# Five unused strips of SBUF that move where the tiles of a hybrid decoder layer begin

## The chip, the cores and the metric

The kernel runs on one core of a Trainium2 chip. The metric is the device time of one execution in microseconds (us): lower is better. The kernel before was timed in three runs, median 1544.72 us, from 1542.8 to 1545.76. Everything else that is told of time here was read from one profiled execution of it.

Words used below: TensorE (PE, "the array") multiplies a *stationary* block of up to 128 x 128, which is loaded into it first (a weight load, PEld), with a *moving* block that streams through it; the sum lands in PSUM. VectorE is DVE, ScalarE ACT, GpSimd POOL; SyncE (SP) issues DMAs. All operands of the array lie in SBUF, where each of 128 partitions has its own bytes; "a tile begins at byte b" means byte b of every partition.

## What is computed

One decoder layer on 512 tokens of width 1024, in float32. After a norm, one projection feeds a short gated convolution and a gated linear recurrence (4 heads, chunks of 32 tokens); their outputs go through an output projection and a residual. Then a feed-forward part picks, for each token, 16 of 16384 experts for each of 8 heads, by product keys:

```
h = rmsnorm(x, norm_mix);  proj = h @ w_in
x = x + concat(conv(...), hgrn2(...)) @ w_out
h2 = rmsnorm(x, norm_ffn)
scores = (h2 @ wq) . keys          # 8 heads x 2 halves x 128 keys
expert, gate = 16 best pairs of the two halves, softmax
y = sum over the 128 experts of a token: gate * gelu(h2 . u[expert]) * v[expert]
out = rmsnorm(x + y, norm_f)
```

## The kernel before

The 512 tokens are 4 blocks of 128. Block 0 takes the experts as written: GpSimd gathers the rows of `u` and `v` (`rows`, L671), VectorE multiplies and adds (L677, L685). Blocks 1 to 3 (384 tokens) are computed densely: all 16384 experts in 128 chunks of 128, with a gate that is zero for experts not picked.

The stages, in the order in which the array meets them:

- **Projections** (`proj`, `proj_mm`): 28 units of weights and 4 of `w_v`. Then the recurrence, in small matmuls, and the **output projection** (`out_mm`).
- **Queries and scores** (`query`, `scores`): 16 units, each followed by small float32 matmuls of `q` with `keys`.
- **First half of the dense experts** (`uchunk`): gelu(h2 U^T) for one chunk, 24 matmuls with 384 moving columns into `pa`. Between them stands the **gate stage** (`gate_m`, L652 and L653): 768 matmuls of 128 columns in float16, which make the matrix of gates from one-hot tiles `A`, `B1` and `B2`, and write it to DRAM (`Gd`).
- **Main loop** (`vchunk`, `vmm`): second half, 18 matmuls with 512 moving columns a chunk into six PSUM banks `y`. For its first 41 turns a `uchunk` stands in each turn too; after those it is `vmm` alone.
- At the end the residual and the last norm (`finish`).

Each large float32 product is made of three matmuls on a rounded part (`hi`, type float32r) and a rest (`lo`), by the helper `mm3` (L113 to L115):

```
PE.matmul(out, l[0], r[0], start=first, stop=False)
PE.matmul(out, l[0], r[1], start=False, stop=False)
PE.matmul(out, l[1], r[0], start=False, stop=last)
```

The second argument is the stationary block, the third the moving one. A row of a trace names them the other way round: `y<-whi,wh` has `whi` moving and `wh` stationary. Which tile plays which part differs from stage to stage, and the prediction turns on it:

| stage | matmuls | moving | stationary |
|---|---|---|---|
| projections, queries | 576 + 384 | `hThi/lo`, `h2Thi/lo`, 512 columns | `whi/lo` |
| the projection of v | 96 | `whi/lo`, 512 | `hThi/lo` |
| output projection | 192 | `whi/lo`, 512 | `mhi/lo` |
| first half (`pa`) | 3072 | `h2Thi/lo`, 384 | `whi/lo` |
| gate stage | 768 | `B1`, `B2`, 128, a step of 4 elements | `A`, the same step |
| second half (`y`) | 2304 | `whi/lo`, 512 | `wh`, `wl` |

`whi/lo` are made from a loaded unit `wraw` by `split`: ACT rounds (L97), DVE subtracts (L99). They have four buffers each; `wraw` is a ring of 4, 8, then 12 buffers, which the gathered rows share. In the main loop DVE multiplies a chunk's activations with its gates (L740), and ACT and DVE split the product into `wh` and `wl` (L743, L745).

The tiles lie in pools, one behind the other in the order in which `body` opens them: constants `cst`, `hp` (hT, h2T), `ws` (whi, wlo), `sm` (small vectors), `mp` (gl), and then pools that follow each other in the same place: those of the front part, those of the selection (`kp`, `rs`, `sp`, `s2`), and those of the main loop (`rm`, `vp`). Each tile is padded to a multiple of 32 bytes. So a few short tiles early on shift all that lie behind them. A scheduler sets the order of the instructions; it does so from their dependencies and estimated lengths.

Of the kernel before, what the change touches and what calls it, by code (L numbers as in the profile page):

```python
# [10 lines left out]
F32 = mybir.dt.float32  # L11
F32R = mybir.dt.float32r
F16 = mybir.dt.float16
# [8 lines left out]
P = 128  # L22
T = 512
# [3 lines left out]
H = 8  # L27
NHP = 2 * H
K = 16
# [24 lines left out]
def body(ctx, tc, a):  # L54
    nc = tc.nc
    V, S, G, PE = nc.vector, nc.scalar, nc.gpsimd, nc.tensor

    def sb(name, bufs=1, **kw):
        return ctx.enter_context(tc.tile_pool(name=name, bufs=bufs, **kw))
# [4 lines left out]
    sm = sb("sm", 2)  # L64
# [3 lines left out]
    def const(name, shape, dt=F32):  # L68
        return cst.tile(shape, dt, name=name)
# [4 lines left out]
    gmask = const("gmask", [P, P])  # L74
    scanm = const("scanm", [P, T])
    ones = const("ones", [P, 2])

    def gain(nm, j):
        return prm[:, PRM[nm] + j:PRM[nm] + j + 1]
# [22 lines left out]
    def wunit(src):  # L102
        raw = ring[0]()
        nc.sync.dma_start(out=raw, in_=src)
        return split(raw)
# [6 lines left out]
    def mm3(out, l, r, first, last):  # L112
        PE.matmul(out, l[0], r[0], start=first, stop=False)  # L113
        PE.matmul(out, l[0], r[1], start=False, stop=False)  # L114
        PE.matmul(out, l[1], r[0], start=False, stop=last)  # L115

    hT = (hp.tile([P, ND, T], F32R, tag="hi", name="hThi"), hp.tile([P, ND, T], F32R, tag="lo", name="hTlo"))
    x1d = dr.tile([NB, P, D], F32, name="x1d")
    h2d = dr.tile([P, D], F32, name="h2d")
# [16 lines left out]
    def big(tag, shape, dt=F32):  # L136
        return fp.tile(shape, dt, tag=tag, name=tag)

    # ---- (x * gain)^T; 1 / rms of a token multiplies what the projections give
    xT = [big(t, [P, 2, T]) for t in ("F", "K", "G", "E1")]  # L140
    for t, nm in ((prm, "prm"), (ident, "ident")):
        S.dma_start(out=t, in_=a[nm])
# [10 lines left out]
        V.scalar_tensor_tensor(hT[1][:, dc, :], t, gain("norm_mix", dc), hT[0][:, dc, :].bitcast(F32), op0=OP.mult,  # L153
                               op1=OP.subtract)

    # ---- projections
    def proj_mm(o, w, dc):
        sl = slice(dc * P, (dc + 1) * P)
        mm3(o, (w[0][:, sl], w[1][:, sl]), (hT[0][:, dc, :], hT[1][:, dc, :]), dc == 0, dc == ND - 1)
# [239 lines left out]
            c = conv_c(tb + 1)  # L399
            hgrn_mix(tb, os_)  # L400

    # ---- output projection, residual, ffn norm
    nfb = fp.tile([P, D], F32, tag="v", name="nfb")
    nc.sync.dma_start(out=nfb, in_=a["norm_ffn"].to_broadcast([P, D]))
    x1 = [big(t, [P, 2, D]) for t in ("F", "K")]
# [27 lines left out]
        S.activation(tmp(), res(tb, 0), AF.Square, accum_out=ms[:, 0, tb:tb + 1])  # L433
    po = [ps() for _ in range(NB)]
    wo = {i: wunit(a["w_out"][1, i]) for i in OORD}
    # ---- dense experts, first half: gelu(h2 @ U^T) of one chunk of 128 experts
    def uchunk(c):
        w = wunit(a["u_l"][c])
        o = psA.tile([P, T], F32, tag="a", name="pa")[:, :TD]
        for dc in range(ND):  # L440
            sl = slice(dc * P, (dc + 1) * P)
            mm3(o, (w[0][:, sl], w[1][:, sl]), (h2T[0][:, dc, P:], h2T[1][:, dc, P:]), dc == 0, dc == ND - 1)
        gl = mp.tile([P, TD], F32, tag="gl", name="gl", bufs=LAG + 1)
        S.activation(gl, o, AF.Gelu)  # L444
        if c < SPILL:
            S.dma_start(out=Ad[c], in_=gl)
        return gl
# [35 lines left out]
    wq0 = [wunit(a["wq"][i]) for i in range(2)]  # L483
    front.close()

    # ---- product keys
    kp = sb("kp")
    e_i32 = kp.tile([P, H * K], I32, name="e_i32")
    gate0 = kp.tile([P, H * K], F32, name="gate0")
# [9 lines left out]
    sp = sel.enter_context(tc.tile_pool(name="sp", bufs=1))  # L499
# [5 lines left out]
    keys = sp.tile([P, NHP, NK], F32, name="keys")  # L505
    S.dma_start(out=keys, in_=a["keys"])
    iota4 = sp.tile([P, NK, 4], F16, name="iota4")
    S.dma_start(out=iota4, in_=a["iota4"])
    iota16 = sp.tile([P, K], F16, name="iota16")
    S.dma_start(out=iota16, in_=a["iota16"])  # L510
    topv = [sp.tile([P, H, 2, K], F32, name="tv%d" % tb) for tb in range(NB)]
    topi = [sp.tile([P, H, 2, K], U32, name="ti%d" % tb) for tb in range(NB)]
# [1 line left out]
    def top16(src, n, vout, iout):  # L514
        V.max(vout[:, 0:8], src)
        V.max_index(iout[:, 0:8], vout[:, 0:8], src)
        r = s2.tile([P, n], F32, tag="mr%d" % n, name="mr")
        V.match_replace(r, vout[:, 0:8], src, LOWEST)
        V.max(vout[:, 8:16], r)
        V.max_index(iout[:, 8:16], vout[:, 8:16], r)  # L520
# [18 lines left out]
            top16(s[:, tb, :], NK, topv[tb][:, i // 2, i % 2, :], topi[tb][:, i // 2, i % 2, :])  # L539

    def pick(tbs):
        """the 16 best pairs of keys of each head: gates and places of both keys.
        A pair (a, b) of the sorted keys has (a + 1) * (b + 1) - 1 others before it, so 50 pairs are all there are."""
        n = len(tbs) * H
        cf = sp.tile([P, len(tbs), H, K], F16, tag="cf", name="cf")
        gs = []
        for j, tb in enumerate(tbs):
            v1, v2 = topv[tb][:, :, 0, :], topv[tb][:, :, 1, :]
            cand = s2.tile([P, H, NCAND], F32, tag="B2", name="cand")
            for a0, st, m in ((0, 0, 16), (1, 16, 8), (2, 24, 5), (3, 29, 4), (4, 33, 3)):  # L550
                V.tensor_add(cand[:, :, st:st + m], v2[:, :, 0:m], v1[:, :, a0:a0 + 1].to_broadcast([P, H, m]))
            V.tensor_add(cand[:, :, 36:42].rearrange("p h (x y) -> p h x y", y=2),
                         v1[:, :, 5:8].unsqueeze(3).to_broadcast([P, H, 3, 2]),
                         v2[:, :, 0:2].unsqueeze(2).to_broadcast([P, H, 3, 2]))
            V.tensor_add(cand[:, :, 42:50], v1[:, :, 8:16], v2[:, :, 0:1].to_broadcast([P, H, 8]))
            cv = s2.tile([P, H, K], F32, tag="cv", name="cv")
            ci = s2.tile([P, H, K], U32, tag="ci", name="ci")
            for h in range(H):
                top16(cand[:, h, :], NCAND, cv[:, h, :], ci[:, h, :])
            g = sp.tile([P, H, K], F32, tag="g%d" % j, name="g")  # L560
            V.tensor_sub(g, cv, cv[:, :, 0:1].to_broadcast([P, H, K]))
            S.activation(g, g, AF.Exp)
            gsum = sp.tile([P, H], F32, tag="gsum", name="gsum")
            V.tensor_reduce(gsum, g, axis=AX.X, op=OP.add)
            V.reciprocal(gsum, gsum)
            V.tensor_mul(g, g, gsum.unsqueeze(2).to_broadcast([P, H, K]))
            gs.append(g.rearrange("p h k -> p (h k)"))
            V.tensor_copy(cf[:, j, :, :], ci)
        cf = cf.rearrange("p j h k -> p (j h k)")
        pa = sp.tile([P, n * K], F16, tag="pa", name="pa")  # L570
        pb = sp.tile([P, n * K], F16, tag="pb", name="pb")
        for j, (st, stp) in enumerate(zip(STARTS, STEPS)):
            m2 = s2.tile([P, n * K], F16, tag="B1", name="m2")
            if j:
                m = s2.tile([P, n * K], F16, tag="A", name="m")
                V.tensor_scalar(m, cf, float(st), None, op0=OP.is_ge)
                V.tensor_add(pa, pa, m)
            else:
                V.tensor_scalar(pa, cf, float(st), None, op0=OP.is_ge)
            V.tensor_scalar(m2, cf, float(st), float(stp), op0=OP.is_ge, op1=OP.mult)  # L580
            V.tensor_sub(pb, pb if j else cf, m2)
        V.scalar_tensor_tensor(pa, cf, -34.0, pa, op0=OP.add, op1=OP.max)
        V.scalar_tensor_tensor(pb, cf, 42.0, pb, op0=OP.is_lt, op1=OP.mult)
        return pa, pb, gs
# [43 lines left out]
    stg = {}  # L628

    def gate_m(tb, b):  # L630
        """gate matrix of 16 tokens: G[i1, i2] per token"""
        r = gt[tb]

        def view(j):
            return r[:, j, b * 16:(b + 1) * 16].rearrange("p (q t) -> p q t", t=4).unsqueeze(2).to_broadcast(
                [P, 4, NK, 4])
        io = iota4[:, None, :, :].to_broadcast([P, 4, NK, 4])
        A = s2.tile([P, 4, NK, 4], F16, tag="A", name="A")
        B1 = s2.tile([P, 4, NK, 4], F16, tag="B1", name="B1")
        B2 = s2.tile([P, 4, NK, 4], F16, tag="B2", name="B2")  # L640
        V.tensor_tensor(A, io, view(0), OP.is_equal)
        V.tensor_tensor(B1, io, view(1), OP.is_equal)
        V.tensor_mul(B2, B1, view(3))
        V.tensor_mul(B1, B1, view(2))
        if b % 2 == 0:
            stg[0] = s2.tile([P, NK // 4, 4, CH], F32, tag="stg", name="stg")
        st = stg[0].rearrange("p g c t -> p t (g c)")
        for q in range(4):
            o = ps()
            o3 = o.rearrange("p (t i) -> p t i", t=4)  # L650
            for t in range(4):
                PE.matmul(o3[:, t, :], A[:, q, :, t], B2[:, q, :, t], start=True, stop=False)  # L652
                PE.matmul(o3[:, t, :], A[:, q, :, t], B1[:, q, :, t], start=False, stop=True)  # L653
            t0 = (b % 2) * 16 + q * 4
            S.activation(st[:, t0:t0 + 4, :], o3, AF.Copy, scale=1.0 / GSC)  # L655
        if b % 2 == 1:
            blk = (tb - 1) * 4 + b // 2
            S.dma_start(out=Gd[:, :, blk].rearrange("g p c t -> p g (c t)"),
                        in_=stg[0].rearrange("p g c t -> p g (c t)"))
# [5 lines left out]
            scores(i - 1, prev)  # L665
        prev = q
    scores(NHP - 1, prev)
    # ---- block 0: rows of its experts gathered
    def rows(tab, j):
        t = ring[0]()  # L670
        G.indirect_dma_start(out=t, out_offset=None, in_=a[tab],  # L671
# [48 lines left out]
        gls[SPILL + k] = uchunk(SPILL + k)  # L720
    sel.close()

    # ---- main loop
    psY = sb("psY", 1, space=PSUM)
    raw_ring(sb("rm", 1), MRING)
    vp = sb("vp", 2)
# [49 lines left out]
        take(k)  # L776
    take(len(slots))

    # ---- residual and last norm
    nfb = vp.tile([P, D], F32, name="nfb", bufs=1)  # L780
    S.dma_start(out=nfb, in_=a["norm_f"].to_broadcast([P, D]))

# [76 lines left out]
```

## Time and profile before

| | us |
|---|---|
| median of three runs | 1544.72 |
| span of the profiled execution, first to last instruction | 1540.5 |
| TensorE busy in it | 1517.9 (99%) |
| VectorE busy | 1212.7 (79%) |
| ScalarE busy | 638.6 (41%) |
| GpSimd busy | 368.8 (24%) |

How to read it: the profile gives, for each instruction, its start and its end. A matmul's end is modelled and lies well behind the start of the next one, since matmuls follow each other in the array before the one ahead has left it. So "busy 99%" only says that the array was never left without work for long. How fast it works is read from starts: the distance from one matmul's start to the next one's is called its *pace* below.

### The profile page before, as it was taken

The page shows a single profiled execution, that of the slowest core. Times are in us where ns is not written, and L with a number is a line of the kernel's source. Part 1 is how long each engine was busy: PE and PEld are TensorE (multiplying, and loading weights), DVE is VectorE, ACT ScalarE, POOL GpSimd, SP SyncE. Part 2 cuts the span into 40 slices and gives each one's busy share as a digit, 9 for nine tenths or more (in the row PEclk, how much of TensorE's full clock was granted, in tenths as well). Part 3 has the DMA queues.
Part 4 walks back from the last instruction along what each step waited for, and adds up shares of the span by engine and source line. Part 5 has one row for each costly group of instructions (what it writes and reads, how often), then busy time and mean ns, then how long its engine had stood idle before and what let it go on. Part 6 is the DMA issues. An engine that isn't in the chain of part 4 may idle for free.

```text
span 1540.5 us, 21785 instructions
## 1 busy us (share of the span) xinstructions
PE 1517.9 (99%) x7929; PEld 1337.1 (87%) x7929; DVE 1212.7 (79%) x2312; ACT 638.6 (41%) x900; POOL 368.8 (24%) x300
## 2 busy tenths in 40 slices
PE   7999999999999999999999999999999999999997
PEld 6887777889999999999999998989898888888886
DVE  5846875899999987876738787777888788878787
ACT  5833334333443456466643333333333333333333
POOL 0000000000053231322014444444343233333340
PEclk9999999999999999999999999999999999999999
DMA  6221234523479787788679998999999999999983
GB/s 231 86 92 56 82 112 162 187 83 117 163 251 373 264 251 252 242 271 269 209 236 412 354 333 303 330 336 326 329 326 364 340 342 353 340 347 346 327 313 138
DMA packets 164653, 394.75 MB, mean 256 GB/s; under 512 B 13249, under 2 KB 84417, under 8 KB 164417
## 3 DMA queue, kind: packets, MB, share of 16 engines
q1 hardware_dynamic: 47520, 170.94, 30.7%
q0 software_dynamic: 41472, 159.40, 28.7%
q10 hardware_dynamic: 75552, 63.01, 12.8%
q8 instruction: 62, 1.02, 0.3%
q14 instruction: 47, 0.38, 0.1%
HBM read 346.90 MB, written 46.40 MB: 255 GB/s over the span
## 4 chain that ended last, share of the span: by engine, by line
PE 93%; DMA 2%; DVE 2%; ACT 1%; issue 1%; POOL 0%; ACTq 0%; DVEq 0%; SPq 0%; POOLq 0%
PE y L113 12%; PE y L114 12%; PE y L115 12%; PE pa L115 10%; PE pa L113 10%; PE pa L114 10%; PE pm L113 6%; PE pm L115 6%; PE pm L114 6%; PE pm L652 3%; PE pm L653 3%; PE pm L535 1%; PE pm L299 1%; DMA wraw<-in_u_dram,e_i 1%; DVE wlo L99 1%; DMA wraw<-in_v_l_dram 1%
## 5 line engine op out<-in xcount | busy, mean ns | idle before, releaser
L97 ACT ACTIVATE whi<-wraw 128x1024 fp32r<-128x1024 f32 x308 | 325.8, 1058 | 514.2 <-PE pa L114 197.9
L99 DVE TENSOR_TENSOR wlo<-wraw,whi 128x1024 fp32r<-128x1024 f32 x308 | 377.1, 1224 | 160.7 <-ACT whi L97 158.5
L113 PE MATMUL pa<-h2Thi,whi 128*128 128x384 f32 x1024 | 345.3, 337 | 2.5 <-ACT gl L444 2.5
L115 PE MATMUL pa<-h2Thi,wlo 128*128 128x384 f32 x1024 | 344.9, 337 | 0.3 <-DVE wlo L99 0.3
L114 PE MATMUL pa<-h2Tlo,whi 128*128 128x384 f32 x1024 | 344.5, 336 | 0.0
L114 PE MATMUL y<-wlo,wh 128*128 128x512 f32 x768 | 304.3, 396 | 0.0
L115 PE MATMUL y<-whi,wl 128*128 128x512 f32 x768 | 304.0, 396 | 0.0
L113 PE MATMUL y<-whi,wh 128*128 128x512 f32 x768 | 303.7, 397 | 0.0
L671 POOL DMA_INDIRECT wraw<-in_u_dram,e_i x128 | 174.9, 1366 | 492.5 <-DMA Ad<-gl 178.5
L671 POOL DMA_INDIRECT wraw<-in_v_dram,e_i x128 | 171.8, 1342 | 301.1 <-DVE wlo L99 136.9
L113 PEld LDWEIGHTS pa<-h2Thi,whi 128*128 128x128 f32 x1024 | 192.8, 188 | 6.0 <-ACT gl L444 3.7
L114 PEld LDWEIGHTS pa<-h2Tlo,whi 128*128 128x128 f32 x1024 | 192.8, 188 | 1.8
L115 PEld LDWEIGHTS pa<-h2Thi,wlo 128*128 128x128 f32 x1024 | 192.7, 188 | 0.9 <-DVE wlo L99 0.6
L115 PEld LDWEIGHTS y<-whi,wl 128*128 128x128 f32 x768 | 144.7, 188 | 35.4
L685 DVE SCALAR_TENSOR_TENSOR y<-wraw,w,y 128x1024 f32<-128x1024 f32 x128 | 163.8, 1280 | 13.8 <-DMA wraw<-in_v_dram,e_i 13.7
L743 ACT ACTIVATE wh<-w 128x384 fp32r<-128x384 f32 x128 | 67.1, 524 | 258.6 <-PE y L114 199.0
L113 PEld LDWEIGHTS y<-whi,wh 128*128 128x128 f32 x768 | 144.6, 188 | 33.2
L114 PEld LDWEIGHTS y<-wlo,wh 128*128 128x128 f32 x768 | 144.5, 188 | 33.2
L677 DVE SCALAR_TENSOR_TENSOR wraw<-wraw,h2n 128x1024 f32<-128x1024 f32 x128 | 155.9, 1219 | 18.7 <-DMA wraw<-in_u_dram,e_i 18.7
L745 DVE TENSOR_TENSOR wl<-w,wh 128x384 fp32r<-128x384 f32 x128 | 71.1, 556 | 53.0 <-ACT wh L743 52.6
L655 ACT ACTIVATE stg<-pm 128x512 f32<-128x512 f32 x96 | 94.3, 1161 | 19.5 <-PE pm L653 19.1
L652 PE MATMUL pm<-B,A 128*128 128x128 f16 x384 | 91.1, 296 | 0.2 <-ACT stg L655 0.2
(242 smaller groups left out, 1817.7 us busy)
## 6 DMA issues: line engine op xcount, KB each, us to landing
wraw<-in_u_l_dram SPq DMA_DIRECT2D x128, 512.0 KB, 5.3
wraw<-in_v_l_dram SPq DMA_DIRECT2D x128, 512.0 KB, 6.5
Gd<-stg ACTq DMA_DIRECT2D x12, 2048.0 KB, 9.9
Gt<-Gd POOLq DMA_DIRECT2D x32, 768.0 KB, 8.2
Ad<-gl ACTq DMA_DIRECT2D x84, 192.0 KB, 4.5
glr<-Ad ACTq DMA_DIRECT2D x84, 192.0 KB, 5.9
wraw<-in_w_in_dram SPq DMA_DIRECT2D x24, 512.0 KB, 3.7
wraw<-in_wq_dram SPq DMA_DIRECT2D x16, 512.0 KB, 8.3
```

What stands on the lines that cost most here:

```text
L97: S.activation(hi, src, AF.Copy)
L99: V.tensor_sub(lo, src, hi.bitcast(F32))
L113: PE.matmul(out, l[0], r[0], start=first, stop=False)
L114: PE.matmul(out, l[0], r[1], start=False, stop=False)
L115: PE.matmul(out, l[1], r[0], start=False, stop=last)
L652: PE.matmul(o3[:, t, :], A[:, q, :, t], B2[:, q, :, t], start=True, stop=False)
L655: S.activation(st[:, t0:t0 + 4, :], o3, AF.Copy, scale=1.0 / GSC)
L671: G.indirect_dma_start(out=t, out_offset=None, in_=a[tab], in_offset=bass.IndirectOffsetOnAxis(ap=e_i32[:, j:j + 1], axis=0))
L677: V.scalar_tensor_tensor(r, r, 1.0, h2n, op0=OP.mult, op1=OP.mult, accum_out=act0[:, j:j + 1])
L685: V.scalar_tensor_tensor(y0, r, w0[:, j:j + 1], y0, op0=OP.mult, op1=OP.add)
L743: S.activation(wh, w, AF.Copy)
L745: V.tensor_sub(wl, w, wh.bitcast(F32))
```

## The change

Five edits, none of which adds or removes an instruction, a wait or a transfer: two tiles that nothing reads or writes, and two tiles that are made wider than what is used of them. (Comments go as well; they move the line numbers by up to 2.)

```diff
     ones = const("ones", [P, 2])
+    const("pad", [P, 48])
...
+    sm.tile([P, 104], F32, name="pad", bufs=1)
     hT = (hp.tile([P, ND, T], F32R, tag="hi", name="hThi"), ...
...
-    iota16 = sp.tile([P, K], F16, name="iota16")
+    iota16 = sp.tile([P, K + 240], F16, name="iota16")[:, 0:K]
...
-            gsum = sp.tile([P, H], F32, tag="gsum", name="gsum")
+            gsum = sp.tile([P, P], F32, tag="gsum", name="gsum")[:, 0:H]
```

The built programs of both kernels have the same 13955 instructions in the same order on every engine, with the same semaphores and the same values waited for. What differs is where tiles begin. As a remainder after division by 512 bytes:

| tiles | before | after |
|---|---|---|
| `hThi/lo`, `h2Thi/lo`, `whi/lo` | 320 | 0 |
| `mhi/lo`, and all other tiles of the front part but `tmp` | 416 | 0 |
| `wraw`, `gl`, `h2n`, `y0`, `keys`, `glr`, `Gt`, `w` | 416 | 0 |
| `wh`, `wl` | 416 | 0 |
| `A`, `B1`, `B2`, `q`, `oh` | 224 | 256 |
| `stg`, `gt` | 160 | 192 |

The slices that a matmul reads begin at multiples of 512 bytes within their tile, so these remainders are those of the operands; only in the gate stage the four slices of a tile begin 0, 2, 4 and 6 bytes further on.

## Rows read from the trace of the kernel before

**Rows 1.** The page: span, busy us of each engine (share) and instructions, the chain by engine.
```profile
span 1540.5 us, 21785 instructions
...
PE 1517.9 (99%) x7929; PEld 1337.1 (87%) x7929; DVE 1212.7 (79%) x2312; ACT 638.6 (41%) x900; POOL 368.8 (24%) x300
...
PE 93%; DMA 2%; DVE 2%; ACT 1%; issue 1%; POOL 0%; ACTq 0%; DVEq 0%; SPq 0%; POOLq 0%
```

**Rows 2.** The waits of TensorE: waiter, releaser: total us, times, longest us.
```profile
PE pm L113 <- ACT whi L97: 8.3, 1, 8.3
PE pm L466 <- DVE h2s L459: 3.2, 2, 3.0
PE pa L113 <- ACT gl L444: 2.5, 2, 1.5
```

**Rows 3.** Windows, TensorE alone: stretch, length, busy (matmuls), granted clock, DMA share, GB/s.
```profile
60.00:78.00 18.00, 18.00 (x81) 1.00 0.34 115
216.00:236.00 20.00, 20.00 (x87) 1.00 0.16 54
410.00:426.00 16.00, 16.00 (x95) 1.00 0.55 172
1300.00:1320.00 20.00, 20.00 (x87) 1.00 0.92 333
820.00:840.00 20.00, 20.00 (x105) 1.00 1.03 408
```

**Rows 4.** Timeline of 60 to 78, projection of v: start, length (us), instruction.
```profile
59.70 0.39 PE L115 MATMUL pm<-whi,hTlo 128*128 128x512 f32 x1
...
77.83 0.39 PE L114 MATMUL pm<-wlo,hThi 128*128 128x512 f32 x1
```

**Rows 5.** Timeline of 216 to 236, output projection.
```profile
215.68 0.39 PE L113 MATMUL pm<-whi,mhi 128*128 128x512 f32 x1
...
235.83 0.40 PE L115 MATMUL pm<-whi,mlo 128*128 128x512 f32 x1
```

**Rows 6.** Timeline of 410 to 426, first half of the experts.
```profile
409.67 0.33 PE L113 MATMUL pa<-h2Thi,whi 128*128 128x384 f32 x1
...
425.96 0.33 PE L114 MATMUL pa<-h2Tlo,whi 128*128 128x384 f32 x1
```

**Rows 7.** Timeline of 1300 to 1320, second half of the experts.
```profile
1299.69 0.40 PE L113 MATMUL y<-whi,wh 128*128 128x512 f32 x1
...
1319.84 0.40 PE L115 MATMUL y<-whi,wl 128*128 128x512 f32 x1
```

**Rows 8.** Groups of TensorE by form: instruction, shapes, count | busy us, mean ns | idle.
```profile
L114 PE MATMUL y<-wlo,wh 128*128 128x512 f32 x768 | 304.3, 396 | 0.0
...
L114 PE MATMUL pm<-wlo,mhi 128*128 128x512 f32 x64 | 25.2, 396 | 0.0
...
L114 PE MATMUL pm<-wlo,hThi 128*128 128x512 f32 x32 | 12.4, 389 | 0.0
```

**Rows 9.** Timeline of the gate stage around 704.
```profile
704.02 0.29 PE L652 MATMUL pm<-B,A 128*128 128x128 f16 x1
704.14 0.41 PE L653 MATMUL pm<-B,A 128*128 128x128 f16 x2
...
704.96 0.30 PE L653 MATMUL pm<-B,A 128*128 128x128 f16 x1
```

**Rows 10.** Scores: the timeline around 325 (eight merged), and their group by form.
```profile
325.27 1.05 PE L535 MATMUL pm<-keys,q 128*128 128x128 f32 x8
...
L535 PE MATMUL pm<-keys,q 128*128 128x128 f32 x128 | 16.9, 275 | 0.0
```

**Rows 11.** Windows, all engines: PE, PEld, DVE, ACT, POOL busy (count), clock, DMA share, GB/s.
```profile
1200.00:1500.00 300.00, 300.00 (x1282) 241.17 (x1281) 243.11 (x321) 105.87 (x146) 102.73 (x93) 1.00 0.94 340
```

**Rows 12.** Groups of VectorE by form.
```profile
L99 DVE TENSOR_TENSOR wlo<-wraw,whi 128x1024 fp32r<-128x1024 f32 x308 | 377.1, 1224 | 160.7 <-ACT whi L97 158.5 <-PE pm L535 1.5
...
L677 DVE SCALAR_TENSOR_TENSOR wraw<-wraw,h2n 128x1024 f32<-128x1024 f32 x128 | 155.9, 1219 | 18.7 <-DMA wraw<-in_u_dram,e_i 18.7
```

## The prediction

> **What bounds the kernel now.** First the page: the array is busy for 1517.9 of 1540.5 us, and 93% of the chain that ended last is its own work [rows 1]. Next the waits, to see whether it is really work: the array waited 8.3 us at the start for the first weights, and then 3.2 and 2.5 us in two more places; these are its three longest sums [rows 2]. So no queue, transfer or other engine sets the time, and a change that moves no instruction can only act through the pace of the matmuls themselves.
>
> So the pace is read next, from starts, in four stretches that hold one kind of matmul each; the counts are those of the windows, and all four ran at a granted clock of 1.00, the level of 2.4 GHz [rows 3].
> - Projection of v: 81 matmuls of 512 columns, first start 59.70, last 77.83: 18.13 / 80 = 226.6 ns [rows 3, 4].
> - Output projection: 87 of 512 columns: (235.83 - 215.68) / 86 = 234.3 ns [rows 3, 5].
> - First half of the experts: 95 of 384 columns: (425.96 - 409.67) / 94 = 173.3 ns [rows 3, 6].
> - Second half: 87 of 512 columns: (1319.84 - 1299.69) / 86 = 234.3 ns [rows 3, 7].
>
> Two things come out. The difference of 226.6 and 173.3 for 128 columns is 0.416 ns a column, one cycle of 2.4 GHz. So a matmul of either width costs its columns and a constant: 226.6 - 213.3 = 13.3 ns, and 173.3 - 160.0 = 13.3 ns. And the output projection and the second half pay 21.0 ns, 7.7 ns more, though their shape and type are those of the projection of v. The mean lengths say the same: 396 ns for `y` and for the output projection, 389 for the projection of v [rows 8].
>
> What sets the two kinds apart? The moving operand is `whi/lo` in all three of the 512-column stretches, at 320 past a multiple of 512. The stationary one begins at 320 for the projection of v (`hThi/lo`), at 416 for the other two (`mhi/lo`, `wh`, `wl`). 320 is a multiple of 64, 416 is 32 past one. Other load is not the cause: the output projection is slow at a DMA share of 0.16, the projection of v fast at 0.34, and the second half slow, to the same tenth of a nanosecond, at 0.92 [rows 3].
>
> **The change, part by part.** The two strips take every fp32r operand to 0 past 512; then stationary and moving begin alike, as they do now in the projection of v. No instruction, wait or transfer is added or moved, so all else costs nothing of itself.
>
> *Second half of the experts.* 2304 matmuls, of which 768 are in the group shown (three such groups [rows 8]). From 234.3 to 226.6: 2304 x 7.7 = 17.7 us. All of it lies on the path: the array does not wait there [rows 2].
>
> *Output projection.* 192 matmuls, 192 x 7.7 = 1.5 us.
>
> *Projections, queries, first half.* 576 + 384 + 96 + 3072 = 4128 matmuls whose operands begin at a multiple of 64 already. That 0 past 512 is better still, no row shows; I take nothing. Bounds: at best all of the 13.3 ns, 54.9 us. At worst they lose what the 32 bytes cost elsewhere, 7.7 ns, 31.8 us; I see no ground for that, since both operands keep their distance to each other.
>
> *Gate stage.* 768 matmuls of 128 columns, nine starts from 704.02 to 704.96: 0.94 / 8 = 118 ns [rows 9]. 128 columns take 53 ns, so it is the load of the next stationary block that sets this pace. Both operands go from 224 (32 past a multiple of 64) to 256. The trace has no gate matmul at another place. The nearest row of 128 x 128 that is held up by as many columns is that of the scores: eight merged in 1.05 us, one is 0.275, so (1.05 - 0.275) / 7 = 111 ns [rows 10]. I take 118 - 111 = 7 ns, also close to the 7.7 above: 768 x 7 = 5.4 us. Bounds: 0, if the step of four elements is what costs, and 118 - 107 = 11 ns, 8.4 us, if the load comes down to 128 columns at half the array's rate (128 / 1.2 GHz).
>
> *The small float32 matmuls* of recurrence and scores stand at 111 ns, 107 of which are columns by the same sum: under 4 ns times some 400, at most 1.6 us, taken as 0.
>
> *Who is late next?* In the second half a chunk is 18 matmuls, 4.22 us now, 4.08 after. VectorE is busy 243.11 of 300 us there [rows 11], 0.81 x 4.22 = 3.42 us a chunk: 84% after, it still fits. The transfers run at 340 GB/s [rows 11], which becomes 340 x 4.22 / 4.08 = 352; they reach 408 at 820 to 840, where the DMA share stands at 1.03, full [rows 3]. So they fit as well; only in some 40 us after 800 could the array be held up, which might cost 1 to 2 us.
>
> The sum: 17.7 + 1.5 + 5.4 = 24.6 us off the profiled 1540.5, so 1515.9 of span. The median lies 4.2 us above that span, for what is outside it and for the spread of the runs; I keep that: 1520.1 us.
>
> **The rivals.**
>
> *Nothing changes* (the change does not do what it says). That would need the 7.7 ns to have another cause than the place, one that the output projection and the second half share and the projection of v lacks. Both slow stages have stationary tiles that were freshly written by ACT and DVE, but so has the projection of v. The time would be 1544.7, with a little less for the gates. [...] Chance 7%.
>
> *The constant goes too.* The 13.3 ns that remain might themselves come from beginning at 320, for instance if what is read at once is longer than 64 bytes; 512 would then help every fp32r matmul. At most all goes: 2304 x 21.0 + 192 x 21.0 + 4128 x 13.3 = 48.4 + 4.0 + 54.9, with 5.4 for the gates 112.7 us, 1432; a fifth of the constant (2.7 ns on 6624 matmuls, 17.9 us) would give 1502; half of it, 44 us, 1476. Against it: no row shows an operand at any third place, and the constant is equal for 384 and 512 columns, so it looks like a turn-around between matmuls. VectorE would still fit at half (3.42 of 3.96 us). [...] Chance 13%, of which 5 near the fifth.
>
> *Slower.* Now `wraw` begins at 416 and `whi/lo` at 320; after, all begin alike, so the rounding and subtracting (L97, L99) read and write in step. If that held VectorE up, the main loop could become its own: from 3.42 us a chunk it passes today's 4.22 when every operation there is 23% longer. At 30%, and with its share of 0.81 taken for the whole loop (2304 x 234.3 ns and 41 x 24 x 173.3 ns, 710 us), the loop takes 0.81 x 1.3 = 1.053 of today's, 38 us more; less 7 us won in the output projection and the gates: 1576. Against it: L677 reads and writes `wraw` with `h2n`, all at 416, and takes 1219 ns; L99, with two places, 1224 [rows 12]. Being in step costs nothing there. Chance 3%.
>
> *Half.* The place helps, but only the part that comes from the load, or the transfers bind: 8 to 12 us off, 1533 to 1537. Chance 5%.
>
> **How the numbers follow.** The forecast has 72%: 1514 to 1529, from the gates' bounds (0 to 8.4 us), the small matmuls and 2 us for transfers. The range is to leave out 2 in 10 at most: up to 1531 and down to 1500 it takes in the forecast and the fifth of the constant, 77%, and with 1535 as its upper end most of the half as well, 81%. So 1500 to 1535. A measurement of this kernel can tell about 0.2%, 3 us. Faster by more than that: 72 + 13 + 5 = 90%; within: 7%; slower: 3%.
>
> **What would show it.** Right: the groups of `y` and of the output projection at 389 ns instead of 396; the window from 1200 holds some 1323 matmuls in 300 us instead of 1282; the first half stays at 173.3; the gate stage comes to 107 to 113 ns; the array's waits stay as they are. The forecast falls if `y` stays at 234 (the place is not the cause), if the first half comes under 172 (the constant depends on it), if waits of the array on DVE, ACT or DMA appear in the main loop, or if the groups of VectorE grow.

## The result, and the profile after

The changed kernel took 1531.5 us (median of 4 runs, 1528.5 to 1533.96) against 1544.08 for the kernel before on the same chip: a ratio of 0.9917, interval 0.9898 to 0.9935. Two later sets of runs gave 0.9888 (0.9869 to 0.9907) and 0.990 (0.9876 to 0.9924). So it is faster by about 1%, 13 to 16 us, where 24.6 were forecast. The 1531.5 us lie within the stated range of 1500 to 1535, near its upper end, and above the 1514 to 1529 that the forecast itself was given. Of the runs that are told of below, one of seven of the kernel with one strip took 1575.65 us at a granted clock of 0.918 and is left out of its ratio.

The page of its profiled execution, lines as in [rows 1]:

```profile
span 1526.7 us, 21785 instructions
...
PE 1502.8 (98%) x7929; PEld 1338.8 (88%) x7929; DVE 1213.2 (79%) x2312; ACT 638.8 (42%) x900; POOL 365.1 (24%) x300
...
PE 91%; DVE 5%; DMA 2%; ACT 1%; issue 1%; POOL 0%; DVEq 0%; ACTq 0%; SPq 0%; POOLq 0%
```

The span fell by 13.8 us, the busy time of the array by 15.1. That of the other engines is what it was, to 4 us. Next the groups of TensorE by form (instruction, shapes, count | busy us, mean ns | idle), as in [rows 8], with those of the first half and of the gate stage:

```profile
L115 PE MATMUL y<-wlo,wh 128*128 128x512 f32 x768 | 299.3, 390 | 0.0
...
L115 PE MATMUL pm<-wlo,mhi 128*128 128x512 f32 x64 | 24.8, 389 | 0.0
...
L114 PE MATMUL pa<-h2Thi,whi 128*128 128x384 f32 x1024 | 346.5, 338 | 4.1 <-ACT gl L446 4.1
...
L654 PE MATMUL pm<-B,A 128*128 128x128 f16 x384 | 91.3, 297 | 0.0
```

`y` and the output projection came down from 396 to 389 or 390 ns. The window from 1200 to 1500 us (columns as in [rows 11]) and starts in it (start, length, instruction) say the same:

```profile
1200.00:1500.00 300.00, 300.00 (x1326) 248.47 (x1325) 251.79 (x329) 109.87 (x150) 103.53 (x93) 1.00 0.96 350
```

```profile
1299.80 0.39 PE L115 MATMUL y<-wlo,wh 128*128 128x512 f32 x1
...
1302.97 0.39 PE L114 MATMUL y<-whi,wh 128*128 128x512 f32 x1
```

1326 matmuls instead of 1282, and fourteen paces from 1299.80 to 1302.97: 226.4 ns. The gates did not move: two of their starts, 18 matmuls apart, give 2.12 / 18 = 118 ns, as in [rows 9].

```profile
699.73 0.30 PE L654 MATMUL pm<-B,A 128*128 128x128 f16 x1
...
701.85 0.30 PE L654 MATMUL pm<-B,A 128*128 128x128 f16 x1
```

All starts of both traces, put together by kind (the time from each start to the next, summed, in us), tell where the 13.8 us come from:

| kind | before | after | difference | forecast |
|---|---|---|---|---|
| `y` | 539.3 | 523.7 | -15.6 | -17.7 |
| output projection | 45.5 | 44.2 | -1.3 | -1.5 |
| gates | 87.2 | 87.3 | +0.1 | -5.4 |
| first half (`pa`), its waits included | 544.8 | 548.4 | +3.6 | 0 |
| projections, queries, v | 248.2 | 247.8 | -0.4 | 0 |

The 3.6 us of the first half lie in one place. Before, the array waited there for 1.5 us [rows 2]; the waits of TensorE after (waiter, releaser: total us, times, longest us):

```profile
PE pm L114 <- ACT whi L98: 8.2, 1, 8.2
PE pa L114 <- ACT gl L446: 4.1, 2, 3.1
```

Windows of after at that place (columns as in [rows 11]):

```profile
450.00:455.00 5.00, 1.91 (x12) 1.59 (x10) 5.00 (x13) 3.03 (x4) 4.09 (x4) 0.92 0.65 206
455.00:460.00 5.00, 5.00 (x16) 5.00 (x17) 5.00 (x14) 1.44 (x2) 3.80 (x4) 0.50 0.88 275
```

The array stands for 3.1 us and then runs 5 us at a granted clock of 0.50: 16 matmuls in them, where before there were 31 in the same window, at 1.00:

```profile
455.00:460.00 5.00, 5.00 (x31) 5.00 (x30) 5.00 (x16) 1.93 (x3) 4.08 (x4) 1.00 0.94 329
```

The timelines of ACT and DVE tell who is late:

```profile
445.24 1.28 ACT L564 ACT_TABLE_LOAD   x1 [0.39 <-ACT gl L446]
451.85 0.31 ACT L564 ACTIVATE g<-g 128x128 f32<-128x128 f32 x1 [5.33 <-DVE g L563]
...
454.42 0.49 ACT L446 ACTIVATE gl<-pa 128x384 f32<-128x384 f32 x1
```

```profile
444.72 1.23 DVE L679 SCALAR_TENSOR_TENSOR wraw<-wraw,h2n 128x1024 f32<-128x1024 f32 x1 [1.60 <-DMA wraw<-in_u_dram,e_i]
...
447.63 1.23 DVE L679 SCALAR_TENSOR_TENSOR wraw<-wraw,h2n 128x1024 f32<-128x1024 f32 x1 [1.38 <-DMA wraw<-in_u_dram,e_i]
...
451.55 0.27 DVE L563 TENSOR_TENSOR g<-cv 128x128 f32<-128x128 f32 x1
```

ACT's queue holds an exponential of the selection (L564) ahead of the `gl` that frees a bank of the first half. It waits 5.33 us for VectorE, whose queue mixes gathered rows (L679) with the steps of the selection that lead to that `g`, and stands for the rows' transfers. The changed kernel does none of this faster.

### The profile page after: what moved, and what is told of

Its sections match the earlier page's. It is cut to its first block, busy times and chain, and to the rows that moved or that the text cites. A ratio compares the mean times of both kernels' runs of the same rounds, so it can differ in the third digit from the quotient of the medians.

```text
span 1526.7 us, 21785 instructions
## 1 busy us (share of the span) xinstructions
PE 1502.8 (98%) x7929; PEld 1338.8 (88%) x7929; DVE 1213.2 (79%) x2312; ACT 638.8 (42%) x900; POOL 365.1 (24%) x300
## 3 DMA queue, kind: packets, MB, share of 16 engines
q8 instruction: 62, 1.02, 0.3%
## 4 chain that ended last, share of the span: by engine, by line
PE 91%; DVE 5%; DMA 2%; ACT 1%; issue 1%; POOL 0%; DVEq 0%; ACTq 0%; SPq 0%; POOLq 0%
PE y L115 11%; PE y L116 11%; PE y L114 11%; PE pa L114 10%; PE pa L116 10%; PE pa L115 10%; PE pm L114 6%; PE pm L115 6%; PE pm L116 6%; PE pm L654 3%; PE pm L655 3%; DVE wlo L100 1%; PE pm L537 1%; DMA wraw<-in_u_dram,e_i 1%; PE pm L301 1%; DMA wraw<-in_v_l_dram 1%
## 5 line engine op out<-in xcount | busy, mean ns | idle before, releaser
L100 DVE TENSOR_TENSOR wlo<-wraw,whi 128x1024 fp32r<-128x1024 f32 x308 | 376.6, 1223 | 155.0 <-ACT whi L98 139.5
L116 PE MATMUL y<-whi,wl 128*128 128x512 f32 x768 | 299.4, 390 | 0.0
L115 PE MATMUL y<-wlo,wh 128*128 128x512 f32 x768 | 299.3, 390 | 0.0
L114 PE MATMUL y<-whi,wh 128*128 128x512 f32 x768 | 297.9, 389 | 0.0
L673 POOL DMA_INDIRECT wraw<-in_u_dram,e_i x128 | 167.5, 1309 | 482.4 <-DMA Ad<-gl 178.4
L673 POOL DMA_INDIRECT wraw<-in_v_dram,e_i x128 | 175.4, 1370 | 303.5 <-DVE wlo L100 134.4
L679 DVE SCALAR_TENSOR_TENSOR wraw<-wraw,h2n 128x1024 f32<-128x1024 f32 x128 | 155.8, 1219 | 15.2 <-DMA wraw<-in_u_dram,e_i 15.2
```

The source lines that it names most:

```text
L100: V.tensor_sub(lo, src, hi.bitcast(F32))
L673: G.indirect_dma_start(out=t, out_offset=None, in_=a[tab], in_offset=bass.IndirectOffsetOnAxis(ap=e_i32[:, j:j + 1], axis=0))
L679: V.scalar_tensor_tensor(r, r, 1.0, h2n, op0=OP.mult, op1=OP.mult, accum_out=act0[:, j:j + 1])
```

## The experiments

The forecast rested on a *place*: operands are read fast from a multiple of 64 bytes. The rival that came up with the result is a *distance*: what counts is how far the stationary tile's start lies from the moving one's, as a remainder, and alike is fast. Below, a pace is the mean distance of consecutive starts of `y` behind 1165 us, where nothing else runs on the array. The kernels of this section ran on several chips. There the kernel before took 1544.92 us (beside one_strip, wh32 and all32), 1545.88 (scan, gate_flat; one run), 1539.97 (wh256, mv32, gate_st, gate_mv; one run) and 1543.97 (gate_swap and the third set of the changed kernel). Eight kernels, wh32, all32, scan, wh256, mv32, gate_flat, gate_st and gate_mv, were run once, so the argument rests on their paces and not on their times.

**The kernel after once more** (after_again).

> The changed kernel once more, beside the one-strip kernel and in more rounds, since its four runs so far lie between 1528.5 and 1534. Theory 'place' and theory 'distance' both expect the same paces as in its first profile (y and output projection 227 ns, first half 173 ns, gates 118 ns). Open is the wait of the array near 452 us: if it is an accident of one execution, the median is 1529 and the wait falls back to 2 us; if it belongs to the kernel, it is 3 us again, with a stretch at half the clock behind it, and the median stays at 1531.

Ratio 0.9888 (0.9869 to 0.9907), span 1529.1. `y`, output projection and gates as above to 0.2 us. The wait at 452 us is there again, 4.0 us long, with another of 1.0 at 656: `pa` 550.1 us.

**One strip of 32 bytes** (one_strip), in the kernel before:

```diff
+    sm.tile([P, 8], F32, name="pad", bufs=1)
     hT = (hp.tile([P, ND, T], F32R, tag="hi", name="hThi"), ...
```

> The kernel before with a single unused strip of 32 bytes behind the small vectors: mhi/lo, wh, wl go from 416 to 448 past a multiple of 512, A and B from 224 to 256, while hT, h2T and whi/lo stay at 320. All operands of the array then begin at multiples of 64, none of the large ones at a multiple of 512. Theory 'place' (a stationary operand that begins off a multiple of 64 costs some 7.7 ns): y and output projection at 227 ns, time as the changed kernel, 1531 us. Theory 'distance' (moving and stationary must begin at the same remainder): distance 128 instead of 96, y stays at 234, 1544 us. Theory '512' (only a multiple of 512 helps): y at 234, 1544 us.

Ratio 0.996 (0.9945 to 0.9975). The pace of `y` is 232.4 ns, its group:

```profile
L114 PE MATMUL y<-wlo,wh 128*128 128x512 f32 x768 | 302.5, 394 | 0.0
```

All operands stand at multiples of 64, and most of the 7.7 ns (5.8) are still paid. The place as forecast is refuted. So is the expectation that `y` stays at 234: 128 bytes cost less than 96, 232.4 against 234.3 ns.

**Only `wh`, `wl` (and `glr`) 32 bytes on** (wh32), in the kernel after:

```diff
+        vp.tile([P, 8], F32, name="pad", tag="pad", bufs=1)
         wh = vp.tile([P, TD], F32R, tag="wh", name="wh", bufs=4)
```

> The changed kernel with wh and wl alone (and glr behind them, which the array does not read) moved on by 32 bytes: one part undone. Both 'place' and 'distance' expect y at 234 ns again, all other paces as in the changed kernel, so 2304 x 7 = 16 us more: 1543 to 1547 us. If the gain came from the transfers, VectorE or ScalarE, which are as in the changed kernel but for these tiles, y stays at 227 ns and the time at 1531.

1541.19 us. `y` goes to 233.3 ns, the output projection stays as after (44.2 us):

```profile
L115 PE MATMUL y<-wlo,wh 128*128 128x512 f32 x768 | 303.6, 396 | 0.0
...
L115 PE MATMUL pm<-wlo,mhi 128*128 128x512 f32 x64 | 24.8, 389 | 0.0
```

So the stationary tile's start carries the gain of `y`. Place and distance both foresee this.

**All operands 32 bytes on** (all32), in the kernel after:

```diff
-    const("pad", [P, 48])
+    const("pad", [P, 56])
```

> The changed kernel with one strip 32 bytes longer at the front: every operand begins 32 bytes further on, all at 32 past a multiple of 64, and all distances between operands stay 0. Theory 'place': every fp32r matmul pays: y, projections and queries 234 ns, first half 181 ns, 6624 x 7.5 = 50 us more than the changed kernel, 1580 us. Theory 'distance': nothing changes against the changed kernel: 227 and 173 ns, 1531 us.

1527.44 us; `y` 226.7 ns, all other kinds as after.

```profile
L115 PE MATMUL y<-wlo,wh 128*128 128x512 f32 x768 | 299.3, 390 | 0.0
```

Here no large operand stands at a multiple of 64, and no kind is slower than in the changed kernel. For `y` it is the distance, and neither 512 nor 64 as a place.

**Eight distances in one kernel** (scan): the buffers of `wh` and `wl` at 64, 128, 192 and so on, `whi/lo` at 0; `hTlo` and `h2Tlo` at 256, `B1` and `B2` 128 and 256 further than `A`.

> The changed kernel with strips that put each buffer of wh and wl at its own distance from the moving tile: wh at 64, 192, 320 and 448, wl at 128, 256, 384 and 480 past a multiple of 512, turn by turn; the moving whi/lo stay at 0. hTlo and h2Tlo lie at 256 while hThi, h2Thi and whi/lo stay at 0, so that one matmul in three of the projections and of the first half has its next stationary block 256 bytes from the moving tile. In the gate stage B1 lies 128 and B2 256 bytes from A. The built order of the instructions is unchanged. Theory '0 is best' (any distance costs): all y matmuls at 231 to 235 ns, the affected third of the first half near 178 to 181 ns, time near before's, 1545 us. Theory 'the cost falls with distance and may go below that of 0': the paces go down from 234 at 64 to 96 over 232 at 128 towards 227 or less at 192 to 320, and the first half's third comes under 173 ns.

1539.28 us, span 1537.5, `y` 532.9 us in all, 231.4 ns on average. Sorted by the distance of the stationary block that comes next, the means of `y` behind 1165 us lie between 228.3 ns (at 128) and 234.5 (at 448); none comes under 226, so the 13.3 ns stay at every distance. The distance alone does not set these paces: from a matmul whose stationary block is at 64 to one at 64 it took 235.8 ns, and to one at 128 it took 228.3. So the scan gives no pace for a distance that all matmuls share. At 256 `y` showed 231.4 beside neighbours of other distances, while projections (227.3), queries (227.4) and `pa` paid nothing at 256. The gates stayed at 117 to 119.

**A uniform 256** (wh256), in the kernel after, the pad ahead of `wh` 64 elements wide:

> The changed kernel with wh, wl and glr all moved to 256 past a multiple of 512, whi and wlo at 0: the uniform distance is 256 in y, where the scan had it mixed with other distances (231.4 ns there). If the distance counts to 512: y 231 to 232 ns, 2304 x 4.5 = some 10 us more than the changed kernel, span 1534 to 1539. If it counts to 256 only (the scan's 231 then came from the neighbours of another distance, and its pa, projections and queries at 256 showed no cost): y 226.7 ns, span 1524 to 1530.

1529.03 us, `y` 226.7 ns:

```profile
L115 PE MATMUL y<-wlo,wh 128*128 128x512 f32 x768 | 299.3, 390 | 0.0
```

So 256 is as good as 0 where all `wh` and `wl` stand there; the scan's slower matmuls at 256 owe it to neighbours.

| kernel | moving at | stationary at | distance | pace of `y`, ns |
|---|---|---|---|---|
| before | 320 | 416 | 96 | 234.3 |
| wh32 | 0 | 32 | 32 | 233.3 |
| one_strip | 320 | 448 | 128 | 232.4 |
| after | 0 | 0 | 0 | 226.7 |
| all32 | 32 | 32 | 0 | 226.7 |
| wh256 | 0 | 256 | 256 | 226.7 |

**The distance in the stages ahead** (mv32): `hT` and `h2T` moved to 32, `whi/lo` kept at 0.

```diff
-    const("pad", [P, 48])
+    const("pad", [P, 56])
...
+    ws.tile([P, 120], F32, name="pad", tag="pad", bufs=1)
```

> The changed kernel with hT and h2T (both halves of each) moved to 32 past a multiple of 512, while whi and wlo stay at 0 and wh, wl, m stay at 0. So the distance from the moving tile's start to the next stationary block's start becomes -32 in the projections, the queries and the first half (pa), +32 in the v-projection, and stays 0 in the output projection and y. Theory (distance, any stage): the scan's matmuls at the distance 480 started 230.8 to 232.9 ns apart instead of 226.7, so pa goes from 173.3 to some 177 to 180 ns, projections and queries to 231 to 233, the v-projection to 233 (wh32's pace); 3072 x 5 ns + 900 x 5 ns = some 20 us, of which the waits of the first half may hide a part: span 1535 to 1548. Rival (only the stages whose moving tile is wh, wl or m are touched, since in the scan the distance 256 cost nothing in pa and the projections): all paces as in the changed kernel, span 1524 to 1530. y and the output projection stay at 227 under both.

1531.41 us, span 1529.6, below the 1535 to 1548 that the distance was to bring. Projections and queries went to 233.4 ns, v to 233.3, as the distance has it; a group of v, 389 ns before [rows 8]:

```profile
L117 PE MATMUL pm<-wlo,hThi 128*128 128x512 f32 x32 | 12.6, 395 | 0.0
```

`pa` did both. Around 412 us it stayed at 173.3 ns, from two of its starts, 24 matmuls apart. In the main loop it did not, 23 matmuls apart:

```profile
411.78 0.34 PE L117 MATMUL pa<-h2Tlo,whi 128*128 128x384 f32 x1
...
415.94 0.34 PE L117 MATMUL pa<-h2Tlo,whi 128*128 128x384 f32 x1
```

```profile
950.17 0.34 PE L116 MATMUL pa<-h2Thi,whi 128*128 128x384 f32 x1
...
954.24 0.34 PE L118 MATMUL pa<-h2Thi,wlo 128*128 128x384 f32 x1
```

That is 4.07 / 23 = 177.0 ns. The 23 paces of such a group in the changed kernel:

```profile
947.60 0.33 PE L114 MATMUL pa<-h2Thi,whi 128*128 128x384 f32 x1
...
951.61 0.33 PE L116 MATMUL pa<-h2Thi,wlo 128*128 128x384 f32 x1
```

They are 4.01 / 23 = 174.3 ns. From 850 to 1160 us the means are 176.8 (mv32) and 174.4 (changed kernel). So 384 columns pay for the distance as well, 2.4 ns, but not in every stretch. The sum hides it: in all `pa` took 545.9 us here, no more than in the changed kernel, since mv32 shows no half clock there: its matmuls keep 177 ns up to 457.57 us, and the first one behind its wait of 1.72 us lasts 0.44 us, where that of the changed kernel lasts 0.69. Why the same tiles at the same distance show two paces is open.

A side result of the same kind: `y` between first-half matmuls stood at 226.6 ns here; in the changed kernel, where over a third of these start 230 to 236 ns apart, it is 229.1. The slow ones are among the first nine behind each change from `pa` to `y`; one such change in the changed kernel:

```profile
951.78 0.39 PE L114 MATMUL y<-whi,wh 128*128 128x512 f32 x1
...
953.87 0.39 PE L114 MATMUL y<-whi,wh 128*128 128x512 f32 x1
...
955.68 0.39 PE L116 MATMUL y<-whi,wl 128*128 128x512 f32 x1
```

Nine paces in 2.09 us are 232.2 ns each, and the next eight, in 1.81 us, 226.3; over all changes the means are 231.2 and 226.7. All these operands begin at 0, so the distance alone does not fix the pace.

**The gates.** First with both operands read as 128 contiguous elements (gate_flat), then the stationary alone (gate_st), then the moving alone (gate_mv, shown for `B2`; `flat` gives 128 neighbouring elements):

```diff
-                PE.matmul(o3[:, t, :], A[:, q, :, t], B2[:, q, :, t], start=True, stop=False)
+                PE.matmul(o3[:, t, :], A[:, q, :, t], flat(B2, q, t), start=True, stop=False)
...
```

> The changed kernel in which the gate stage's matmuls read 128 neighbouring elements of the same tiles A, B1 and B2 in place of every fourth one; so the matrix of gates that they make is another, and the output with it. All else is the same. Theory 'the step of four sets the 118 ns' : 107 ns or less, 768 x 11 = 8 us less than the changed kernel, down to 60 ns and 45 us less if float16 blocks without a step load faster; then the stage may wait for VectorE or ScalarE instead. Theory 'the load of 128 columns sets it': 118 ns stays, 1529 us.

> The changed kernel with the gate matmuls' stationary operand A read as 128 contiguous elements instead of every fourth; the moving operands B1 and B2 keep their step of 4. (The gate matrix that comes out is another one: work and transfers are the same.) With both contiguous the matmuls started 56 ns apart instead of 118. If the step costs in the weight load: some 56 ns here, span 1521 to 1525. If it costs in the moving read: 118 ns here, span 1524 to 1530. If in both: between 56 and 118.

> The changed kernel with the gate matmuls' moving operands B1 and B2 read as 128 contiguous elements instead of every fourth; the stationary operand A keeps its step of 4. (The gate matrix that comes out is another one: work and transfers are the same.) If the step costs in the weight load: 118 ns here, span 1524 to 1530. If it costs in the moving read: 56 ns here, span 1521 to 1525. If in both: between 56 and 118.

1523.76, 1527.48 and 1522.2 us. The groups of gate_st and, behind it, of gate_mv:

```profile
L657 PE MATMUL pm<-B,A 128*128 128x128 f16 x384 | 89.6, 293 | 0.0
```

```profile
L657 PE MATMUL pm<-B,A 128*128 128x128 f16 x384 | 49.9, 223 | 4.6 <-ACT stg L660 4.5
```

From starts: 118 ns as changed, 116 with the stationary operand contiguous, 56 with the moving one, 56 with both. Two starts of gate_mv, 18 matmuls apart (1.01 / 18 = 56 ns):

```profile
699.81 0.22 PE L657 MATMUL pm<-B,A 128*128 128x128 f16 x1
...
700.82 0.22 PE L658 MATMUL pm<-B,A 128*128 128x128 f16 x1
```

The moving operand's step of four elements sets the pace. But 42 us less of gates (45.0 instead of 87.4) shorten the span by little, for the array then waits; gate_mv:

```profile
PE pa L114 <- ACT gl L446: 25.7, 15, 4.1
```

The first half takes 36.0 us more than in the changed kernel (584.4 instead of 548.4). Of these, 21.6 are longer waits for `gl`. The granted clock is lower as well: 0.98 from 500 to 850 us in gate_mv, and 0.93 in each of the three windows of 50 us from 600 to 750 in gate_flat, where the changed kernel has 1.00.

**A version meant to keep that gain** (gate_swap): `A` and `B` change sides, `A` is written contiguous and moves, and the chunks are cut by the other key; beside it the changed kernel for a third time.

```diff
-                PE.matmul(o3[:, t, :], A[:, q, :, t], B2[:, q, :, t], start=True, stop=False)
+                PE.matmul(o3[:, t, :], B2[:, q, :, t], A[:, q, t, :], start=True, stop=False)
...
```

> A version of the changed kernel with the same output that keeps the gain of gate_mv: the two sides of the gate matmuls change places (B1, B2 become the stationary operands, read with a step of 4, A the moving one), A is written with the keys contiguous, so that the moving read has no step, and the chunks of u and v are cut by the first key instead of the second, on the host. Price: A's one VectorE operation per 16 tokens (1221 ns, 24 of them) has a stride of 0 in the innermost dimension of one operand and may take longer; if twice as long, 24 x 1.2 = 29 us of VectorE in the stage from 500 to 850 us, where VectorE is busy 34 of 50 us. Theory (the moving operand's step sets the gates' pace): 56 ns instead of 118, 768 x 60 = 46 us less on the array in that stage, of which gate_mv, with 26 us of waits for gl, kept only some 5 us; with VectorE longer, 0 to 5 us are left: span 1520 to 1530. Rival (VectorE becomes the stage's bound): slower than the changed kernel, 1530 to 1545.

> The changed kernel once more, on the same chip and in the same rounds as gate_swap, so that the two can be set side by side: 1527 to 1533 us; the wait for gl at 452 us shows again, 3 to 5 us from start to start.

It failed: 1573.45 us, a ratio of 1.0178 (1.0156 to 1.02), against 1528.9 us and 0.990 (0.9876 to 0.9924) for the changed kernel beside it. That is longer than either of its two theories had it; the wait for `gl` in the profile beside it was 2.8 us, a little under the 3 to 5 expected. Its gates are fast (46.8 us in all), but VectorE's `A` takes 2287 ns instead of 1221, and the array waits in many places: the first half takes 610.1 us instead of 545.6, `y` 550.5 instead of 523.7, at a mean granted clock of 0.975 instead of 0.996. Its group on VectorE, the waits of TensorE, and ACT's timeline:

```profile
L645 DVE TENSOR_TENSOR A<-iota,gt 128x2048 f16<-128x2048 f16 x24 | 54.9, 2287 | 15.2 <-PE pm L659 8.1 <-ACT gt L627 7.2
```

```profile
PE pa L114 <- ACT gl L446: 21.3, 14, 4.0
PE y L114 <- ACT wh L749: 17.1, 1, 17.1
PE pa L114 <- ACT whi L98: 14.9, 2, 13.8
PE y L115 <- DVE wlo L100: 14.8, 9, 2.8
```

```profile
831.56 0.38 ACTq L664 DMA_DIRECT2D Gd<-stg  x1
832.04 0.49 ACT L446 ACTIVATE gl<-pa 128x384 f32<-128x384 f32 x1 [15.92 <-DMA Gd<-stg]
```

The dearer operation is 25.6 us of VectorE (24 x 1.066). The rest goes together with an order that the scheduler made anew: among other things ACT stands 15.9 us at a transfer of gates to DRAM at 816 us, with the next chunk's work behind it. How the loss divides between these was not taken apart.

## Why the prediction came out as it did

- **What bounds the kernel**: right. No instruction moved, and all of the gain is pace, in the two stages named. The 2.4 GHz beside a granted clock of 1.00 is an estimate, 1 / 0.416 ns; the traces give the clock as a share alone.
- **The second half**: right in kind, 2.1 us short. Where `y` runs alone it came to 226.7 ns as forecast. The missing 2 us lie between first-half matmuls, where it came to 229.1; there the forecast took over a pace from a stretch of one kind. They fall on the first nine matmuls behind each change from `pa` to `y`, at 231.2. With `hT` 32 bytes on they are gone, so they depend on where tiles begin as well; how is open.
- **Output projection, projections, queries, first half**: right in pace, 1.3 us and nothing; the 3.6 us that the first half lost are a wait and the clock behind it.
- **The gates**: wrong, 5.4 us forecast, none measured. The step that failed is the reading that the load of the next stationary block sets this pace, and with it the analogy with the scores, 118 - 111 = 7 ns, by which the place of `A` and `B` was to cost what it costs elsewhere. That 107 of the 111 ns of a float32 matmul are columns is near what the trace of before shows: two of 512 columns (L368, at 133.25 us) last 1.02 us merged and one 0.592, so they start 428 ns apart, and an estimate from 428 and 111 is (428 - 111) / 384 = 0.825 ns a column, 106 for 128. But that is float32, and the float16 gates do not share it: with contiguous operands they take 56 ns (gate_flat), near the 53 of 0.416 ns a column. The lower bound, 0 "if the step of four elements is what costs", is what happened, and gate_mv shows the cause: 62 of the 118 ns.
- **Waits**: wrong by up to 4 us. The text took the array's waits to stay as they are, and looked for what is late next only in the main loop. The wait at 452 us, 1.5 us in the profile of before, was 3.1, 4.0 and 2.8 in three profiles of after. That the array comes there earlier, while VectorE's chain of gathered rows keeps its time, would explain it: mv32, whose projections are slower, waits 1.7. But one_strip waits 2.8 with the output projection nearly as slow as before, so the growth lies within what the place varies by from profile to profile; whether the change makes it longer is not settled. The half clock behind the wait is seen in after (0.50) and after_again (320 ns from start to start); one_strip went on at 173 ns behind its 2.8 us. Over all runs whose clock is on record the mean granted clock was 0.9940 in 14 runs of after, against 0.9956 in 19 of before. An estimate from these two, 0.0016 x 1530 us, is 2.4 us that the clock takes back from the gain. The runs of after spread with it, from 1522.95 us at 0.998 to 1533.96 at 0.992. Which wait causes it in each run is not on record.
- **The explanation**: the number was right and the reason wrong. The text had both in hand, 320 and 320 against 320 and 416, and chose the multiple of 64 for its terms over "stationary and moving begin alike"; for this change both give the same time, since all tiles go to 0. So it was luck that the wrong reason gave the right term for `y`. The kernel with one strip shows what the wrong choice would have cost: by the forecast's reason it should have brought nearly all of the gain, and it brought under half of it (5.4 of 15.6 us in the same rounds).
- **The sum**: 10.8 us too much off the span: gates 5.4, first half 3.6, `y` 2.1, output projection 0.2, less small differences elsewhere. The median of 1531.5 us lies between the forecast's own 1514 to 1529 and the 1533 to 1537 of *Half*; it is within the range because that was widened for *Half*, and *Half* named the load or the transfers as its reason, which is not what happened. The other rivals did not come: no pace came below the constant of 13.3 ns at any distance tried, VectorE's groups kept their lengths (L100 1223 ns, L679 1219), and something did change.

## What to carry to other kernels

When matmuls of one shape run at two paces, read each from starts and compare where the stationary and the moving tile begin relative to each other before padding anything: here equal starts (or 256 bytes apart) gave the fast pace for 512 columns in steady runs of them, from every place tried (0, 32 and 320 past a multiple of 512). Read a step inside a moving operand as a cost of its own (here 62 of 118 ns). And a stage that gets faster must be checked for the queue that feeds it: of the 42 us off the gates, 36 came back in the first half, most of them as waits.

## What the runs showed of the hardware that was not expected

- **The pace of 512-column fp32r matmuls depends on the distance between the two operands' starts**: 226.7 ns at 0 and 256, 233.3 at 32, 234.3 at 96, 232.4 at 128. Six kernels here show that the pace is not free of where the two begin; what makes it so, no run shows.
- **384 columns show it only in part**: at -32 they ran at 173.3 ns around 412 us, as at 0, and at 177.0 in the main loop, where at 0 they ran at 174.3.
- **The distance alone does not fix the pace**: with all operands at 0, the first nine paces of `y` behind `pa` were 231.2 ns on average, and the next eight 226.7. What sets them is open.
- **A step of 8 bytes in a moving float16 operand doubles the time**: 118 against 56 ns for 128 columns; in the stationary one it costs 2 at most.
- **VectorE's comparison of 2048 float16 elements took 2287 ns instead of 1221** in gate_swap, where `A` is laid out anew and one operand has a stride of 0 in its innermost dimension; that of `B1`, left as it was, took 1219 there. No run has the stride alone.
